# A planner's priorities and engine choices replaced by a table, in a two-layer hybrid attention trunk

## The chip, the core and the metric

One NeuronCore of a Trainium2 chip runs the whole program. The metric is the device time of one execution in microseconds (us); three runs of the kernel before gave 615.03, 615.44 and 615.48 us, a median of 615.44 us.

## What is computed

The input x is 256 tokens by 1024 channels. Each of two layers normalises x, multiplies it by one wide matrix (1024 by 9808), feeds the columns to three causal token mixers of eight heads each, and adds the merged result to x. A final RMSNorm ends the program. Cut to what matters:

```python
def hybrid_layer(x, gain, w_in, f_bias, w_branch, w_out):
    h = rms_norm(x, gain)
    proj = jnp.einsum('bsd,de->bse', h, w_in)
    (qa, ka, va, ga, qb, kb_, vb_, gb, qc, kc, vc, gc,
     q_idx, k_idx, w_idx, f_logit, merge_logit) = jnp.split(proj, SPLIT_POINTS, axis=-1)
    ...
    oa = moba_attention(rope(qa), rope(ka), va) * silu(ga)
    ob = dsa_attention(rope(qb), rope(kb_), vb_, qi, ki, wi) * silu(gb)   # top 64 keys of an indexer
    oc = forgetting_attention(qc, kc, vc, log_f) * silu(gc)
    y = jnp.einsum('nbsw,nwd->bsnd', jnp.stack([oa, ob, oc], axis=0), w_branch)
    merged = jnp.sum(sigmoid(merge_logit) * y, axis=2)
    return x + jnp.einsum('bsd,de->bse', merged, w_out)
```

With 256 tokens the block attention is plain causal attention over one block.

## The kernel before, in words

All matmuls keep nearly float32 accuracy: every operand is split into a high part (a rounding copy on ScalarE, L402) and a low part (source minus high on VectorE, L406), and each product is three matmuls: high by high, high by low, low by high (L444). Weights come from memory in chunks of up to 1 MB into four `raw` buffers, are split into rings of six `wh` and six `wl` buffers, and go to TensorE as the stationary operand, 128 columns at a time; one "unit" of 24 matmuls makes 128 output channels for all 256 tokens in one PSUM bank. Three banks (`proj`) take units, two (`s`) the attention scores, two (`t`) transposes, one (`o`) the attention outputs.

A layer's units come in this order: v of mixer a, v of mixer c with the index keys, the indexer (with eight rounds of top-8 on VectorE), the pairs of heads of mixer a, of mixer c, of mixer b, with merge gates (`m`) and branch products (`y`) put between them, and at the end the output projection. A pair of heads runs as a chain: scores (L665, L667), bias and row minimum on VectorE (L733, "max"), exp on ScalarE (L737), reciprocal (L740, L741, "recip"), a 16-bit high part of the probabilities (L745 on ScalarE or L748 on VectorE, "p hi"), its low part on VectorE (L752, "p lo"), a transpose by DMA from SyncE's queue (L761), a copy into `pt` (L766 on ScalarE or L767 on VectorE, "pT"), the product with v (L779 to L782, "av"), the sum of its two halves (L795, L797), the gate (L800, "og", on VectorE or GpSimd) and a split (L434, L435). The gate itself is L693 (tanh on ScalarE) and L694 (VectorE, "g"); L694 also sets free the `proj` bank that its unit filled. L977 on VectorE or L978 on GpSimd adds a branch product to the accumulator.

Nothing is ordered at run time but by semaphores. A planner (`Plan.run`) walks through all 3226 operations once, when the program is built: each has a modelled cost, its dependencies, its buffers and a priority (`key`, the smaller the earlier; a unit's number is the base of its operations' keys). At each step it takes the engine that can start soonest and, among that engine's operations that can start within a slack of that moment (0 on TensorE, 110 ns on ScalarE and VectorE, 1500 ns on SyncE), the one with the smallest key. Where an operation may go to two engines (`ways`), it takes the one that ends sooner by its model, after a penalty (500 ns for VectorE at "p hi" and "pT"). The order that comes out is fixed for each engine; an engine that waits holds everything behind it. The transpose is modelled as T_ISSUE on SyncE's queue and T_LAND until the data may be read:

```python
plan.op([("SP", T_ISSUE, tr)], k_hi + k_lo, k_t, key, T_LAND, "pT", touch=[e, t16]).quick = 1400.0
```

At the start, SyncE loads the two halves of the first 128 tokens (`x0`, L998), weights of mixer a's v in eight pieces (`va0` to `va7`, L1057, keys -95 to -93.6) and the two halves of the second 128 tokens (`x1`, L998, keys -94.7 and -94.69). The second half's norm is a sum of squares (L517), a mean (L524), a power on GpSimd (L526), a scaling (L534, L537) and transposes on TensorE (L567).

Of the kernel before, what the change touches and what calls it, by code (L numbers as in the profile page):

```python
# [38 lines left out]
STEP = 24.0  # L39
SPLIT_LEAD = 2.0  # L40
P_SCALE = 32768.0
T_ISSUE = 1400.0
T_LAND = 1600.0
AWAY = 500.0
SLACK = {"PE": 0.0, "ACT": 110.0, "DVE": 110.0, "SP": 1500.0}
MARGIN = 200.0
# [41 lines left out]
    return c  # L88


SHIFT = {}


CUR = [""]
# [21 lines left out]
class Plan:  # L116
# [8 lines left out]
    def op(self, ways, reads, writes, key, lag=0.0, name="", touch=()):  # L125
        o = Op()
        o.ways, o.key, o.lag, o.name, o.margin, o.port, o.half, o.quick = ways, key, lag, name, 0.0, False, False, 0.0
        deps, o.bufs = {}, []
        for t in reads:
            for d in t.w:  # L130
                deps[id(d)] = d
        for t in writes:
            for d in t.w + t.r:
                deps[id(d)] = d
        for t in reads:
            t.r.append(o)
        for t in writes:
            t.w, t.r = [o], []
        for t in {id(t): t for t in list(reads) + list(writes) + list(touch)}.values():
            if isinstance(t, Buf):  # L140
                if t.no is None:
                    t.no = self.made[t.tag] = self.made.get(t.tag, -1) + 1
                t.left += 1
                o.bufs.append(t)
        o.deps = list(deps.values())
        o.n, o.out, o.need, o.end = len(self.ops), [], 0, None
        o.key += SHIFT.get(o.n, 0.0)
        for d in o.deps:
            if d is not o:
                d.out.append(o)  # L150
                o.need += 1
        self.ops.append(o)
        return o
# [111 lines left out]
def hybrid_trunk(ctx, tc, x, w_in, w_branch, w_out, final_gain, consts, out):  # L265
# [15 lines left out]
    def T(b):  # L281
        return b.slot[1]
# [388 lines left out]
    class Pair:  # L671
# [44 lines left out]
        def attend(self, key):  # L716
# [8 lines left out]
            for h in range(2):  # L725
# [34 lines left out]
                def tr(h=h, t16=t16):  # L760
                    nc.sync.dma_start_transpose(T(t16).rearrange("p (a b) -> p a b", a=6), w16()[:, 768 * h:768 * h + 768])  # L761
                plan.op([("SP", T_ISSUE, tr)], k_hi + k_lo, k_t, key, T_LAND, "pT", touch=[e, t16]).quick = 1400.0
                for i in range(2):
# [497 lines left out]
```

## Time and profile before

| what | value |
|---|---|
| runs, median of 3 | 615.44 us |
| the profiled execution, its own time | 613.8 us |
| span in that profile | 612.0 us |
| TensorE busy | 595.2 us (97%) |
| VectorE busy | 543.9 us (89%) |
| ScalarE busy | 471.8 us (77%) |
| GpSimd busy | 87.2 us (14%) |

The span is the profiled part of that execution, 1.8 us shorter than its time. Matmuls overlap in the array, so their busy time counts nearly every instant in which one is under way; it hides waits that are shorter than a matmul's own length. In the rows a name such as `proj<-hTh,wh` says what is written and what is read; "idle before <-X" names the operation whose end released the instruction.

### The profile page before, as it was taken

Reading aid. Unit: us, or ns where it says so; the run is one execution under the profiler, and the core shown is the slowest. Engines: PE = TensorE matmul, PEld = TensorE weight load, DVE = VectorE, ACT = ScalarE, POOL = GpSimd, SP = SyncE. Lnnn points to the kernel's source line nnn. Section 1 sums busy time; section 2 is a strip of 40 time slices with the busy share of each in tenths; the row PEclk is TensorE's granted clock in tenths of the full one; section 3 lists DMA queues with packets and bytes.
Section 4 is the critical chain, followed back from the end, with each engine's and each line's share of the span. In section 5 each row is a group of like instructions: output and inputs, shape, how many; then the busy total and the mean of one; then the engine's idle time right before and its main releaser. Section 6 shows DMA issues by size and latency. Waiting matters only on the chain.

```text
span 612.0 us, 12689 instructions
## 1 busy us (share of the span) xinstructions
PE 595.2 (97%) x4704; PEld 570.4 (93%) x4704; DVE 543.9 (89%) x1342; ACT 471.8 (77%) x1028; POOL 87.2 (14%) x96
## 2 busy tenths in 40 slices
PE   8999999999999999999999999999999999999995
PEld 6899999989898999999889999999999899999985
DVE  8889998988798999899685999999989988999783
ACT  5768668988897779896395775799989876999741
POOL 1013142000000333200000420520000014221000
PEclk9999999999999999999999999999999999999999
DMA  9986285688586746478746645585957696464911
GB/s 314 297 271 189 74 271 110 186 204 263 103 276 170 226 140 168 125 191 309 227 138 207 207 139 159 172 219 128 322 160 224 136 276 195 113 194 88 344 34 70
DMA packets 136509, 116.83 MB, mean 191 GB/s; under 512 B 42752, under 2 KB 127360, under 8 KB 136448
## 3 DMA queue, kind: packets, MB, share of 16 engines
q1 hardware_dynamic: 136160, 115.59, 64.7%
q8 instruction: 37, 0.61, 0.4%
q10 hardware_dynamic: 288, 0.43, 0.2%
q14 instruction: 24, 0.20, 0.1%
HBM read 103.42 MB, written 1.05 MB: 171 GB/s over the span
## 4 chain that ended last, share of the span: by engine, by line
PE 33%; DVE 32%; ACT 19%; DMA 7%; issue 6%; POOL 2%; SPq 0%; POOLq 0%; DVEq 0%; ACTq 0%
PE proj L444 25%; DVE wl L406 10%; ACT wh L402 6%; DMA t<-e 5%; PE proj L1131 4%; DVE e L752 4%; ACT e L737 3%; DVE rsh L493 2%; DVE e L733 2%; DVE isc L907 2%; DVE isc L928 2%; DVE rr L495 1%; ACT pt L766 1%; DMA raw<-in_w_branch_dram 1%; DVE t L927 1%
## 5 line engine op out<-in xcount | busy, mean ns | idle before, releaser
L444 PE MATMUL proj<-hTh,wh 128*128 128x256 f32 x1024 | 266.3, 278 | 0.7 <-DVE bd0l L824 0.2
L444 PE MATMUL proj<-hTl,wh 128*128 128x256 f32 x1024 | 265.2, 277 | 0.0
L406 DVE TENSOR_TENSOR wl<-raw,wh 128x1024 fp32r<-128x1024 f32 x180 | 224.4, 1258 | 13.6 <-ACT wh L402 12.0
L444 PE MATMUL proj<-hTh,wl 128*128 128x256 f32 x1024 | 229.3, 277 | 0.0
L402 ACT ACTIVATE wh<-raw 128x1024 fp32r<-128x1024 f32 x180 | 187.1, 1055 | 37.1 <-PE proj L444 28.6
L444 PEld LDWEIGHTS proj<-hTh,wh 128*128 128x128 f32 x1024 | 192.2, 188 | 2.5 <-DVE g L694 1.3
L444 PEld LDWEIGHTS proj<-hTl,wh 128*128 128x128 f32 x1024 | 192.2, 188 | 0.1
L444 PEld LDWEIGHTS proj<-hTh,wl 128*128 128x128 f32 x1024 | 173.4, 188 | 0.0
L494 POOL TENSOR_TENSOR rsh<-rsh,cst 128x256 f32<-128x256 f32 x40 | 30.1, 752 | 378.7 <-DVE rsh L493 311.6
L496 POOL TENSOR_TENSOR rr<-rr,rsh 128x256 f32<-128x256 f32 x40 | 48.2, 1205 | 4.5 <-DVE rr L495 1.5
L766 ACT ACTIVATE pt<-t 128x384 fp32r<-128x384 f16 x78 | 37.0, 515 | 12.4 <-DMA t<-e 12.2
L737 ACT ACTIVATE e<-e,st 128x128 f32<-128x128 f32 x96 | 42.5, 444 | 2.1 <-DVE st L733 2.1
L752 DVE SCALAR_TENSOR_TENSOR e<-e,st 128x128 f16<-128x128 f32 x96 | 42.0, 437 | 1.0
L745 ACT ACTIVATE e<-e,st 128x128 f16<-128x128 f32 (+1 forms) x92 | 36.7, 443 | 2.4 <-DVE st L741 1.6
L444 PE MATMUL proj<-wh,v 128*128 128x512 f32 (+1 forms) x144 | 35.2, 366 | 0.0
L444 PE MATMUL proj<-og0l,wh 128*128 128x256 f32 x128 | 34.3, 279 | 0.6 <-DVE og0l L435 0.6
L444 PE MATMUL proj<-og0h,wh 128*128 128x256 f32 x128 | 32.9, 281 | 1.6 <-DVE g L694 1.6
L444 PEld LDWEIGHTS proj<-wh,v 128*128 128x128 f32 x144 | 25.3, 189 | 4.2
L444 PE MATMUL proj<-og0h,wl 128*128 128x256 f32 x128 | 28.8, 278 | 0.0
L444 PEld LDWEIGHTS proj<-og0h,wh 128*128 128x128 f32 x128 | 24.1, 188 | 2.1 <-DVE g L694 2.0
L444 PEld LDWEIGHTS proj<-og0l,wh 128*128 128x128 f32 x128 | 24.1, 188 | 1.0 <-DVE og0l L435 1.0
L797 DVE TENSOR_TENSOR ot<-o,ot 64x256 f32<-64x256 f32 x48 | 19.9, 414 | 2.4 <-ACT ot L795 2.0
(224 smaller groups left out, 1069.9 us busy)
## 6 DMA issues: line engine op xcount, KB each, us to landing
raw<-in_w_in_dram SPq DMA_DIRECT2D x74, 1024.0 KB, 5.7
raw<-in_w_branch_dram SPq DMA_DIRECT2D x24, 512.0 KB, 4.1
raw<-in_w_out_dram SPq DMA_DIRECT2D x8, 1024.0 KB, 8.4
raw<-in_x_dram SPq DMA_DIRECT2D x8, 256.0 KB, 5.0
tmp<-wf SPq DMA_DIRECT2D x16, 128.0 KB, 5.2
t<-e SPq DMA_TRANSPOSE x48, 2.8
raw<-in_w_in_dram SPq DMA_DIRECT2D x2, 320.0 KB, 7.6
x<-in_x_dram SPq DMA_DIRECT2D x2, 256.0 KB, 4.3
```

The costliest lines, as they stand in the source:

```text
L402: ACT.activation(p[0].v, sel(c.v), AF.Copy)
L406: DVE.tensor_tensor(p[1].v, sel(c.v), p[0].v.bitcast(F32), op=ALU.subtract)
L444: PE.matmul(o(), a(), b(), start=first and i == 0, stop=last and i == n - 1)
L493: dve(lambda: DVE.stream_shuffle(T(sh)[:np_], a(), SWAP), S, [ps], [sh], key, "rope")
L494: gps(lambda: POOL.tensor_tensor(T(sh)[:np_], T(sh)[:np_], s[:np_], op=ALU.mult), S, [k_rope], [sh], key, "rope")
L496: gps(lambda: POOL.tensor_tensor(T(r)[:np_], T(r)[:np_], T(sh)[:np_], op=ALU.add), S, [sh], [r], key, "rope")
L737: act(lambda t=t, a=a, n=n, st=st, h=h: ACT.activation(ex(h, a, n), ex(h, a, n), AF.Exp, bias=T(st)[:, t:t + 1], scale=-1.0, accum_out=T(s ...
L745: ACT.activation(hi(a, n), ex(h, a, n), AF.Copy, scale=T(st)[:, 4 + t:5 + t])
L752: dve(lambda t=t, a=a, n=n, st=st, h=h, hi=hi, lo=lo: DVE.scalar_tensor_tensor(lo(a, n), ex(h, a, n), T(st)[:, 4 + t:5 + t], hi(a, n), op0 ...
L766: plan.op([("ACT", t_act(384, False), lambda to=to, src=src: ACT.activation(to(), src(), AF.Copy)), ("DVE", t_dve2(384), lambda to=to, src ...
L797: dve(lambda r=r, h=h: DVE.tensor_tensor(T(t)[r], T(o)[:64, h * S:(h + 1) * S], T(t)[r], op=ALU.add), S, [o], [kt[h]], key, "og", touch=[t ...
L1131: PE.matmul(T(ps[t])[:, :w], hA[hi](a + x, t), T(p[wi])[:, ats[w > 256][wi]][:, :n * w].rearrange("p (k c) -> p k c", k=n)[:, x], start=le ...
```

## The change

Two constants of the planner's model of the transposes are smaller. A table SHIFT adds a number between -12 and +6 to the keys of 327 operations (255 earlier, 72 later), named by their number in the order in which the code makes them. A new table WAY adds -1500 or +1500 ns to the modelled cost on VectorE of 53 operations that have two ways: -1500 sends one to VectorE, +1500 to the other engine. No instruction is added or removed; the planner runs anew with these, so any place in any engine's order may move. Cut (the two tables to their first and last lines):

```diff
-T_ISSUE = 1400.0
-T_LAND = 1600.0
+T_ISSUE = 1250.0
+T_LAND = 1500.0
...
-SHIFT = {}
+SHIFT = {
+    0: -11.5, 1: -7, 3: -11.5, 4: -11, 17: 2, 28: -8, 31: -6, 47: -11, 73: 4, 80: -12, 89: -2.5, 90: -11.5, 91: 1.5,
+    98: -8, 99: -9.5, 100: 2.5, 188: 3, 308: -7, 310: -7, 364: 6, 380: 2.5, 386: -12, 387: -7, 419: 3.5, 440: -11,
...
+    2992: -3, 3009: -4, 3044: -12, 3046: -9, 3048: -8, 3076: -12, 3079: -11.5, 3127: -7, 3175: -12, 3177: 6, 3212: 5,
+}
+WAY = {
+    17: -1500, 18: -1500, 90: -1500, 99: 1500, 489: 1500, 490: 1500, 539: 1500, 552: -1500, 553: -1500, 559: 1500,
...
+    2802: 1500, 2827: 1500, 2841: 1500, 2846: -1500, 2852: 1500, 2940: 1500, 3009: -1500,
+}
...
         o.key += SHIFT.get(o.n, 0.0)
+        if len(ways) > 1 and o.n in WAY:
+            o.ways = [w + (WAY[o.n],) if w[0] == "DVE" else w for w in ways]
```

Operations that the prediction names: 0 and 1 are the loads of `x0`, 3 and 4 those of `x1`; 80, 89 and 98 those of `va1`, `va2` and `va3` (`va0`'s load is not in the table); 47 is the mean of the second half's norm; 478, 479, 1380, 1381, 2942 and 2943 are the "max" operations that free score banks at 92.9, 256 and 551 us; 1078, 1079, 2640 and 2641 are the gates "g" ahead of the last branch products of mixer a.

## Rows read from the trace of the kernel before

**Rows 1.** The page: busy time, share and instructions of each engine, and the TensorE clock that was granted, in tenths, over 40 equal slices.

```profile
PE 595.2 (97%) x4704; PEld 570.4 (93%) x4704; DVE 543.9 (89%) x1342; ACT 471.8 (77%) x1028; POOL 87.2 (14%) x96
PEclk9999999999999999999999999999999999999999
```

**Rows 2.** Busy time by stretch: the stretch and its length, then the busy time of each engine in it (with the number of instructions), the granted clock, the share of the DMA engines and their rate.

```profile
50.00:100.00 50.00, 49.38 (x427) 48.81 (x427) 49.03 (x153) 36.40 (x79) 11.91 (x13) 1.00 0.53 153
100.00:150.00 50.00, 48.32 (x414) 46.89 (x413) 45.67 (x105) 43.78 (x98) 3.81 (x4) 1.00 0.77 210
150.00:200.00 50.00, 47.49 (x373) 44.91 (x372) 43.23 (x122) 43.30 (x105) 0.00 (x0) 1.00 0.72 192
...
400.00:450.00 50.00, 49.78 (x437) 49.17 (x436) 47.00 (x106) 45.79 (x101) 3.82 (x4) 1.00 0.79 220
```

**Rows 3.** TensorE's waits: what waited for what, the idle time in us in total, how often, the longest.

```profile
PE o L779 <- ACT pt L766: 2.5, 4, 1.1
PE proj L444 <- DVE g L694: 1.6, 2, 0.8
PE s L665 <- DVE st L733: 1.5, 4, 0.5
PE t L567 <- ACT tmp L534: 1.3, 1, 1.3
...
PE proj L444 <- DVE og0l L435: 0.6, 1, 0.6
PE o L779 <- DVE ot L797: 0.5, 1, 0.5
PE o L781 <- ACT pt L766: 0.3, 1, 0.3
```

**Rows 4.** What a matmul of a unit takes by its record, from the page's groups of instructions (count, then total us and mean ns).

```profile
L444 PE MATMUL proj<-hTh,wh 128*128 128x256 f32 x1024 | 266.3, 278 | 0.7 <-DVE bd0l L824 0.2
```

**Rows 5.** How far matmuls of a unit stand apart when nothing holds them, from the chain that ended last in order of time: start in us, length in us, what, how many.

```profile
35.79 2.76 PE proj L444 x24
```

**Rows 6.** The timeline of the first 17 us, single lines: start, length, engine (SPq is SyncE's queue), line, operation, tiles, shapes, count, and in brackets the idle time before with its releaser.

```profile
0.74 0.87 SPq L998 DMA_DIRECT2D xg<-in_x_dram  x2
1.66 0.90 SPq L1057 DMA_DIRECT2D raw<-in_x_dram  x2
2.60 0.91 SPq L998 DMA_DIRECT2D x<-in_x_dram  x2
3.54 2.95 SPq L1057 DMA_DIRECT2D raw<-in_x_dram  x6
...
7.21 0.50 PE L1071 MATMUL proj<-wh,hTh 128*128 128x512 f32 x1
...
10.73 0.63 ACT L517 ACTIVATE acc<-x 128x512 f32<-128x512 f32 x1
...
14.22 0.15 DVE L524 SCALAR_TENSOR_TENSOR small<-small 128x1 f32<-128x1 f32 x1
...
16.15 0.44 PE L567 MATMUL t<-cst,tmp 128*128 128x128 f32 x2 [1.30 <-ACT tmp L534]
```

**Rows 7.** The page's busy rate of the DMA engines in the first slice of 15.3 us (GB/s, 40 slices).

```profile
GB/s 314 297 271 189 74 271 110 186 204 263 103 276 170 226 140 168 125 191 309 227 138 207 207 139 159 172 219 128 322 160 224 136 276 195 113 194 88 344 34 70
```

**Rows 8.** The timeline around the gate "g" and the branch product that waits for its bank, VectorE and TensorE.

```profile
188.71 0.41 DVE L694 SCALAR_TENSOR_TENSOR g<-th,proj 128x256 f32<-128x256 f32 x1
...
189.18 0.39 PE L444 MATMUL proj<-og0h,wh 128*128 128x256 f32 x1 [0.81 <-DVE g L694]
```

**Rows 9.** The transposes by DMA (L761): durations of their issue in ns, min/median/max, with first and last start, and the time from issue to landing over all 48.

```profile
L761 SPq DMA_TRANSPOSE t<-e x48: 1209/1222/2732, 96.3 to 562.3; - x48
...
DMA to landing us min/median/max: 2.7/2.8/7.1
```

**Rows 10.** Who waited for a transpose to land: idle us in total, times, longest.

```profile
ACT pt L766 <- DMA t<-e: 12.2, 10, 2.2
...
DVE pt L767 <- DMA t<-e: 4.8, 3, 2.5
```

**Rows 11.** Groups of instructions of the operations that can go to either engine: count, then total us and mean ns of one.

```profile
L766 ACT ACTIVATE pt<-t 128x384 fp32r<-128x384 f16 x78 | 37.0, 515 | 12.4 <-DMA t<-e 12.2
...
L745 ACT ACTIVATE e<-e,st 128x128 f16<-128x128 f32 x48 | 18.9, 394 | 2.4 <-DVE st L741 1.6 <-DVE st L740 0.6
...
L800 DVE TENSOR_TENSOR ot<-ot,g 128x256 f32<-128x256 f32 x24 | 10.7, 446 | 0.8
...
L767 DVE CAST pt<-t 128x384 fp32r<-128x384 f16 x18 | 6.1, 355 | 4.8 <-DMA t<-e 4.8
...
L748 DVE TENSOR_SCALAR e<-e,st 128x256 f16<-128x256 f32 x4 | 1.4, 350 | 0.1
```

**Rows 12.** The timeline of VectorE and GpSimd around 207 us: a weight split alone and two beside GpSimd's multiply and add.

```profile
205.79 1.22 DVE L406 TENSOR_TENSOR wl<-raw,wh 128x1024 fp32r<-128x1024 f32 x1
...
207.45 0.73 POOL L494 TENSOR_TENSOR rsh<-rsh,cst 128x256 f32<-128x256 f32 x1 [99.39 <-DVE rsh L493]
207.59 1.68 DVE L406 TENSOR_TENSOR wl<-raw,wh 128x1024 fp32r<-128x1024 f32 x1
208.27 1.61 POOL L496 TENSOR_TENSOR rr<-rr,rsh 128x256 f32<-128x256 f32 x1
...
209.87 1.78 DVE L406 TENSOR_TENSOR wl<-raw,wh 128x1024 fp32r<-128x1024 f32 x1
```

32 rows, old and new, of tables (SHIFT, WAY) are left out of this document.

## The prediction

> **What bounds the kernel now.** I read the page's busy times first. TensorE is busy for 595.2 of 612.0 us at the full clock throughout [rows 1], so neither the clock nor the amount of matmul work leaves much, and the change alters neither. What is left to an order is the time in which TensorE waits. The busy time hides part of that: a matmul's record is 278 ns long [rows 4], but 24 in a row take 2.76 us, 115 ns each [rows 5], so a wait shows as idle only beyond 278 - 115 = 163 ns, and each listed wait is really that much longer.
>
> The list of TensorE's waits [rows 3] then gives the prize. After the head there are the products with v waiting for the transposed probabilities on ScalarE (2.5 and 0.3 us, 5 times), branch products waiting for a gate (1.6, 2 times), scores waiting for the row minimum to free a score bank (1.5, 4 times), and two single waits at the split and the sum of mixer outputs (0.6 and 0.5). That is 7.0 us in 13 waits, with 13 x 0.163 = 2.1 us added 9.1 us. In the head one wait of 1.3 us, really 1.5 us, stands before the second half's transposes. Together 10.6 us: what an order that never lets TensorE wait there could win, and the floor of my range.
>
> Third I read the timeline at these waits. At 189 us a gate on VectorE ends at 188.71 + 0.41 and a branch product that needs its bank starts right behind it, 0.81 us late [rows 8]. In the head the second half's sum of squares ends its main instruction at 10.73 + 0.63 = 11.36 us, but the mean is issued at 14.22 us, because VectorE has it behind weight splits, and TensorE starts the transposes at 16.15 us [rows 6]. So these are matters of place in a queue, not of work. Last I read the stretches: between 100 and 200 us VectorE is busy for 88.9 of 100 us and ScalarE for 87.1, between 50 and 100 us VectorE for 49.03 of 50 [rows 2]; this says how much room a moved operation finds.
>
> **The change part by part.** No instruction is added, so the sum is over waits.
>
> *Head.* The mean (operation 47) gets -11 and both loads of x1 move up. By their keys the loads go x0, x0, va1, x1, x1, va3, va2, va0 in place of x0, x0, va0, va1, x1, x1, va2, va3. The first weight piece comes as early as now, the second two loads later. A load is 256 KB, at the 314 GB/s of the first slice [rows 7] 0.83 us, so the second piece comes 1.7 us later, at a time when the first one feeds TensorE with three matmuls only (about 0.7 us at 0.23 us each, twice the 115 ns of a matmul half as wide). Bounds: a loss of 1.0 us, if the later piece holds TensorE from 7.2 us on [rows 6], and a gain of 1.5 us, if the wait at 16.15 us goes whole. I take a gain of 1.0, nearer to the gain, since the mean has 2.9 us of queueing to give (14.22 - 11.36) and x1 comes one load earlier too.
>
> *Body, priorities.* The shifted operations lie where the waits are: the gates at 187 to 189 us and at 482 to 484 us have -6.5 and -12, the "max" operations that free the score banks at 92.9, 256 and 551 us -2.5 to -12, and many "recip", "p lo" and "pT" steps between 90 and 200 us are in the table. The waits that it addresses are those on the pT copies, on the gates and on the row minimum, the last in three of its four places, which I count as three quarters: 2.8 + 1.6 + 1.1 = 5.5 us in 10 waits, with 10 x 0.163 = 1.6 us added 7.1 us. The fourth score bank, the split and the sum of mixer outputs have no entry. Bounds: nothing, if every operation pulled forward only makes the one it passes late, and 7.1 us. An operation passed on VectorE is in most places a weight split for a unit several us away, which can bear it; but behind a wait that goes, the next dependency is seldom far. I take two thirds, 4.7 us.
>
> *Body, engines.* Laid along the static order, 34 of the 53 assignments name another engine than now: 12 pT copies and 10 "p hi" from ScalarE to VectorE, 2 pT copies the other way, 2 scalings in the head to VectorE, and 6 gates "og" and 2 accumulations to GpSimd. ScalarE loses 10 x 0.51 us of copies net and 10 x 0.39 us at least of "p hi", 9.0 us, and VectorE gains 10 x 0.355 + 10 x 0.35 = 7.1 us [rows 11], both where each has idle time [rows 2]; for TensorE that is nothing by itself. But VectorE now also waits for landings. A pT copy that waits for its transpose cost it 4.8 us in 3 times, 1.6 us each [rows 10], and 18 copies [rows 11] lead to 3 waits. Twelve more make 2 more waits, 3.2 us of VectorE with weight splits and gates queued behind them. Bounds: nothing, where VectorE is ahead, and 3.2 us. I take a third, 1.0 us lost, as VectorE keeps some lead in these stretches.
>
> *GpSimd.* The 8 moved operations take 0.45 us each on VectorE [rows 11], 3.6 us in all. A weight split takes 1.22 us alone and 1.68 or 1.78 us beside GpSimd [rows 12], 0.46 to 0.56 us more, so 8 such meetings cost 3.7 to 4.5 us: about nothing is won or lost, and I count nothing, between a gain of 3.6 us of VectorE (no meeting) and a loss of 0.9. The Trainium skill ("SBUF — State Buffer", section "Who interferes with whom") says that VectorE with two SBUF inputs and GpSimd reading SBUF exclude each other for a whole instruction. By it each move would hold VectorE for GpSimd's whole 0.73 us, 5.8 us in all, and a third of the net 2.2 us would put my time 0.7 us higher; the measured stretching is less, so I go by the rows.
>
> *The two constants.* They put a transpose at 1.25 + 1.5 = 2.75 us in place of 3.0 us; the measured landing is 2.7 at least, 2.8 in the median and 7.1 at most [rows 9]. They move the copies at most 0.25 us forward in the plan; I count nothing for the shortest landings and leave the late ones to the last rival.
>
> The sum: -1.0 - 4.7 + 1.0 = -4.7 us. Against the profiled execution that is 613.8 - 4.7 = 609.1 us; this execution was 1.6 us under the median of 615.4, so the median to expect is **610.7 us**.
>
> **The rivals.**
>
> *All waits go.* The order removes all listed waits: 615.4 - 10.6 = 604.8 us. For it: the shifts stand in the very places of the waits. Against it: three of the waits have no entry near them, and the landings up to 7.1 us do not follow a priority.
>
> *The waits only change places.* An order fixed at build time fits one set of landings and lengths; the gains are eaten by new waits of the same size, and the table does not do what it is for. 615.4, within 1.2 us of it. For it: VectorE at 49.03 of 50 us [rows 2] can't take up a lead from the head, and 7.1 us of work are added to it. Against: ScalarE and VectorE both have idle time in the stretches where most entries lie.
>
> *Slower: VectorE is held by transposes.* The 12 copies given to VectorE are of 9 transposes. If the landing is late for all of them, as an earlier place in the order and the 2.75 us under the median landing [rows 9] would make it, each holds VectorE for 1.6 us [rows 10], 14.4 us in all; half of it, 7.2 us, reaches TensorE through late weight splits and gates. The waits on pT copies then stay (2.8 + 5 x 0.163 = 3.6 us, of which I had counted two thirds, 2.4), so of my gains 5.7 - 2.4 = 3.3 us are left, and the time is 615.4 + 7.2 - 3.3 = 619.3 us. It decides from 3.3 / 9 = 0.4 us of TensorE per transpose on. For it: ScalarE already loses 12.2 us to landings, and a queue in order passes this on. Against: the copies can land later in VectorE's order too, and ScalarE's waits would shrink with them.
>
> **How the numbers follow.** The forecast of 610.7 us (606.5 to 613.8) gets 0.58, all waits gone 0.12, changed places 0.11, VectorE held 0.19. A measurement can tell about 0.2%, 1.2 us, from no change. Faster is the first two, 0.70; same 0.11; slower 0.19. The range goes from 604.3 us, just under the floor of the waits, to 617.5 us, where the head's loss of 1.0 us and some of the last rival are in and its worse part, about 0.1, is out. The forecast alone would span 606.5 to 613.8 us.
>
> **What would show it.** Right: the gates' waits of TensorE are gone, the waits on pT copies and on the row minimum are down to about a third, the mean in the head is issued before 12.5 us, TensorE's last matmul comes some 4 to 5 us earlier, VectorE's busy time is up by about 7 us and ScalarE's down by about 9. The prediction is wrong if the pT copies on VectorE wait over 10 us in all for landings, if the weight splits (L406) become what TensorE waits for, or if the head's first matmuls after 7.2 us stand waiting for a weight piece for over 1 us.

## The result, and the profile after

| | before | after |
|---|---|---|
| median of 4 runs each, same chip | 615.39 us (615.03 to 615.48) | 601.2 us (600.14 to 601.6) |
| the profiled execution: its time, its span | 613.8, 612.0 us | 601.2, 599.4 us |
| TensorE idle in the span | 612.0 - 595.2 = 16.8 us | 599.4 - 587.5 = 11.9 us |

The ratio is 0.9768, with a 95% interval of 0.9751 to 0.9785: 14.2 us faster, where 4.7 us were forecast. Between the two traces the difference is 12.6 us, because the profiled execution of before was 1.6 us under its median and that of after is at its own. The order and the engines of the operations are all that differs; in the code after, lines stand 42 further down (L486 was L444, L821 was L779).

The first lines of the page of after, answering to [rows 1], and of its chain of waits, shares by engine (before it was PE 33%, DVE 32%, ACT 19%, DMA 7%):

```profile
PE 587.5 (98%) x4704; PEld 567.8 (95%) x4704; DVE 542.3 (90%) x1360; ACT 463.8 (77%) x1004; POOL 92.4 (15%) x102
PEclk9999999999999999999999999999999999999999
PE 58%; DVE 22%; ACT 9%; DMA 5%; issue 4%; POOL 0%; SPq 0%; POOLq 0%; DVEq 0%; ACTq 0%
```

The same 4704 matmuls at the same clock have 7.7 us less busy time (595.2 to 587.5), and the idle time fell by only 4.9 us. More than half of the gain thus lies inside what the profile counts as busy. How waits get there can be seen in the busy time by stretch; first before, then after, columns as in [rows 2]:

```profile
0.00:20.00 20.00, 17.55 (x77) 13.54 (x78) 16.10 (x48) 12.82 (x33) 1.81 (x8) 1.00 0.96 317
20.00:100.00 80.00, 79.38 (x658) 78.25 (x657) 75.29 (x199) 57.52 (x117) 18.11 (x20) 1.00 0.66 196
100.00:200.00 100.00, 95.81 (x785) 91.80 (x784) 88.90 (x226) 87.08 (x202) 3.81 (x4) 1.00 0.74 201
```

```profile
0.00:20.00 20.00, 18.54 (x87) 15.43 (x88) 17.83 (x52) 12.43 (x29) 2.06 (x8) 1.00 0.94 313
20.00:100.00 80.00, 80.00 (x677) 79.65 (x676) 74.62 (x208) 58.27 (x118) 19.80 (x22) 1.00 0.67 202
100.00:200.00 100.00, 98.07 (x813) 95.07 (x812) 93.57 (x233) 88.90 (x200) 6.37 (x6) 1.00 0.76 204
```

From 20 to 100 us TensorE was busy for 79.38 of 80 us, so by that column an order could win 0.62 us there; measured by the distances between matmul starts (below), TensorE lost 1.3 us in it before and 0.3 us after. (The counts in brackets, 658 and 677, are not of the same matmuls, as TensorE after is 2.3 us ahead at 20 us.) The timeline of before at 123 us shows how a wait hides. Columns: start, length, engine, line, operation, tiles, shapes, count:

```profile
123.43 0.28 PE L444 MATMUL proj<-hTl,wh 128*128 128x256 f32 x1
123.55 0.28 PE L444 MATMUL proj<-hTh,wl 128*128 128x256 f32 x1
123.94 0.38 PE L444 MATMUL proj<-hTh,wh 128*128 128x256 f32 x1
```

The first two starts are 0.12 us apart, the normal distance [rows 5]; the third comes 0.39 us after the second, so TensorE lost 0.28 us there, but the record of the matmul before fills all of it except 0.11 us, and the row has no bracket with an idle time at all. I therefore took, from all matmul starts in order, each distance less the undisturbed one for that width (0.113 us for 256 columns, 0.058 for 128, 0.226 for 512) and kept what was over 0.07 us. The head is counted from the first transposes on, which start at 6.3 us before and 6.6 us after; what stands ahead of them is warm-up products of `ones`. This is worked out from the traces, not a view of the page:

| time that TensorE lost, us (number of gaps) | before | after |
|---|---|---|
| head, the first 20 us | 4.0 | 1.4 |
| then gaps of 0.07 to 0.163 us, which leave no idle time | 5.0 (48) | 2.3 (22) |
| gaps of 0.163 to 0.3 us | 2.9 (12) | 0.3 (1) |
| gaps over 0.3 us | 9.7 (15) | 5.4 (8) |
| all | 21.6 | 9.3 |

(The entries are rounded one by one.) The difference of the sums, 12.2 us, is nearly the whole 12.6 us between the traces. By what stood waiting, over the whole span: products with v lost 6.7 us before and 2.2 after, branch products 3.6 and 1.6, scores 2.7 and 0.4.

TensorE's listed waits of after, answering to [rows 3]: what waited for what, us in total, times, longest.

```profile
PE proj L486 <- DVE mth L1017: 1.3, 1, 1.3
PE o L821 <- ACT pt L808: 1.1, 3, 0.5
PE t L1032 <- DVE ones L1027: 1.1, 1, 1.1
PE proj L486 <- ACT mth L986: 1.0, 1, 1.0
PE proj L486 <- DVE g L736: 0.3, 2, 0.2
```

The wait for the row minimum and the 1.3 us in the head are gone, that for the gate is down from 1.6 to 0.3 us, that for the pT copies from 2.8 to 1.1. Two single waits for a bank that had not been freed are new: for a merge gate's product with a branch product on VectorE (L1017, 1.3 us) and for a merge gate's tanh on ScalarE (L986, 1.0 us).

The head, answering to [rows 6]: loads in the order x0, x0, va1, x1, x1, then the other pieces, and the mean (L566) at 7.95 us where it was at 14.22.

```profile
1.67 0.42 SPq L1099 DMA_DIRECT2D raw<-in_x_dram  x1
2.13 0.91 SPq L1040 DMA_DIRECT2D x<-in_x_dram  x2
...
7.95 0.15 DVE L566 SCALAR_TENSOR_TENSOR small<-small 128x1 f32<-128x1 f32 x1
```

Last the operations with a choice of engine, answering to [rows 10, 11]: two waits for landings, then groups (count, total us, mean ns, idle before):

```profile
ACT pt L808 <- DMA t<-e: 6.8, 4, 2.9
...
DVE pt L809 <- DMA t<-e: 1.2, 3, 0.7
```

```profile
L808 ACT ACTIVATE pt<-t 128x384 fp32r<-128x384 f16 x73 | 34.3, 513 | 7.1 <-DMA t<-e 6.8
L809 DVE CAST pt<-t 128x384 fp32r<-128x384 f16 x23 | 9.1, 412 | 1.3 <-DMA t<-e 1.2
L842 DVE TENSOR_TENSOR ot<-ot,g 128x256 f32<-128x256 f32 x18 | 7.7, 426 | 0.6
L841 POOL TENSOR_TENSOR ot<-ot,g 128x256 f32<-128x256 f32 x6 | 5.9, 978 | 32.0 <-DVE ot L839 31.9
L790 DVE TENSOR_SCALAR e<-e,st 128x256 f16<-128x256 f32 x10 | 3.4, 351 | 0.1
L790 DVE TENSOR_SCALAR e<-e,st 128x128 f16<-128x128 f32 x9 | 2.5, 282 | 0.0
```

VectorE has 5 more pT copies net and 15 more "p hi" (19 in place of 4), ScalarE as many fewer. Operation by operation 67 changed engine: 40 from ScalarE to VectorE, 17 the other way, 8 from VectorE to GpSimd and 2 back. The table differs from the order of before in 34; the planner moved the other 33 by itself when it ran anew.

The Trainium skill ("Perfetto Trace Analysis", section "Identifying the Most-Contended Engine") says that the busy share of matmuls is no good measure of what is left, and that the busy share of weight loads is one. These traces agree: weight loads left 612.0 - 570.4 = 41.6 us free before and 599.4 - 567.8 = 31.6 us after, 10.0 of the 12.6 us, where matmul idle time shows 4.9.

### The profile page after: what moved, and what is told of

Read it like the earlier page. It is cut to its first block, busy times and chain, and to the rows that moved or that the text cites. A ratio compares the mean times of both kernels' runs of the same rounds, so it can differ in the third digit from the quotient of the medians.

```text
span 599.4 us, 12672 instructions
## 1 busy us (share of the span) xinstructions
PE 587.5 (98%) x4704; PEld 567.8 (95%) x4704; DVE 542.3 (90%) x1360; ACT 463.8 (77%) x1004; POOL 92.4 (15%) x102
## 4 chain that ended last, share of the span: by engine, by line
PE 58%; DVE 22%; ACT 9%; DMA 5%; issue 4%; POOL 0%; SPq 0%; POOLq 0%; DVEq 0%; ACTq 0%
PE proj L486 47%; DVE wl L448 7%; PE proj L1173 4%; DMA t<-e 4%; ACT wh L444 2%; PE proj L1113 2%; DVE isc L970 2%; DVE e L794 1%; DVE rsh L535 1%; ACT pt L808 1%; ACT e L779 1%; DVE t L969 1%; DVE isc L949 1%; DMA raw<-in_w_out_dram 1%; DVE rr L537 1%
## 5 line engine op out<-in xcount | busy, mean ns | idle before, releaser
L486 PE MATMUL proj<-hTh,wh 128*128 128x256 f32 x1024 | 265.7, 278 | 1.5 <-ACT mth L986 1.0
L486 PE MATMUL proj<-hTl,wh 128*128 128x256 f32 x1024 | 265.0, 277 | 0.0
L448 DVE TENSOR_TENSOR wl<-raw,wh 128x1024 fp32r<-128x1024 f32 x180 | 223.3, 1249 | 15.2 <-ACT wh L444 14.0
L486 PE MATMUL proj<-hTh,wl 128*128 128x256 f32 x1024 | 227.9, 276 | 0.0
L444 ACT ACTIVATE wh<-raw 128x1024 fp32r<-128x1024 f32 x180 | 188.7, 1054 | 38.6 <-PE proj L486 26.3
L486 PEld LDWEIGHTS proj<-hTh,wh 128*128 128x128 f32 x1024 | 192.2, 188 | 2.3 <-ACT mth L986 1.2
L486 PEld LDWEIGHTS proj<-hTl,wh 128*128 128x128 f32 x1024 | 192.2, 188 | 0.0
L486 PEld LDWEIGHTS proj<-hTh,wl 128*128 128x128 f32 x1024 | 172.9, 188 | 0.0
L536 POOL TENSOR_TENSOR rsh<-rsh,cst 128x256 f32<-128x256 f32 x40 | 32.4, 812 | 351.4 <-DVE rsh L535 323.2
L538 POOL TENSOR_TENSOR rr<-rr,rsh 128x256 f32<-128x256 f32 x40 | 45.6, 1140 | 2.8
L779 ACT ACTIVATE e<-e,st 128x128 f32<-128x128 f32 (+1 forms) x96 | 42.6, 445 | 2.9 <-DVE st L775 2.4
L794 DVE SCALAR_TENSOR_TENSOR e<-e,st 128x128 f16<-128x128 f32 (+1 forms) x96 | 40.1, 424 | 1.1 <-ACT e L787 0.4
L808 ACT ACTIVATE pt<-t 128x384 fp32r<-128x384 f16 x73 | 34.3, 513 | 7.1 <-DMA t<-e 6.8
L486 PE MATMUL proj<-wh,v 128*128 128x512 f32 (+1 forms) x144 | 35.2, 366 | 0.0
L486 PE MATMUL proj<-og0l,wh 128*128 128x256 f32 x128 | 33.8, 277 | 0.0
L486 PE MATMUL proj<-og0h,wh 128*128 128x256 f32 x128 | 32.4, 278 | 1.3 <-DVE mth L1017 1.3
L787 ACT ACTIVATE e<-e,st 128x256 f16<-128x256 f32 (+1 forms) x77 | 31.6, 445 | 2.7 <-DVE st L783 2.3
L486 PEld LDWEIGHTS proj<-wh,v 128*128 128x128 f32 x144 | 25.3, 189 | 4.3
L486 PE MATMUL proj<-og0h,wl 128*128 128x256 f32 x128 | 28.6, 276 | 0.0
L486 PEld LDWEIGHTS proj<-og0h,wh 128*128 128x128 f32 x128 | 24.0, 188 | 1.6 <-DVE mth L1017 1.5
L486 PEld LDWEIGHTS proj<-og0l,wh 128*128 128x128 f32 x128 | 24.0, 188 | 0.0
L486 PEld LDWEIGHTS proj<-og0h,wl 128*128 128x128 f32 x128 | 21.7, 188 | 0.0
```

What stands on the lines that cost most here:

```text
L444: ACT.activation(p[0].v, sel(c.v), AF.Copy)
L448: DVE.tensor_tensor(p[1].v, sel(c.v), p[0].v.bitcast(F32), op=ALU.subtract)
L486: PE.matmul(o(), a(), b(), start=first and i == 0, stop=last and i == n - 1)
L536: gps(lambda: POOL.tensor_tensor(T(sh)[:np_], T(sh)[:np_], s[:np_], op=ALU.mult), S, [k_rope], [sh], key, "rope")
L538: gps(lambda: POOL.tensor_tensor(T(r)[:np_], T(r)[:np_], T(sh)[:np_], op=ALU.add), S, [sh], [r], key, "rope")
L779: act(lambda t=t, a=a, n=n, st=st, h=h: ACT.activation(ex(h, a, n), ex(h, a, n), AF.Exp, bias=T(st)[:, t:t + 1], scale=-1.0, accum_out=T(s ...
```

## The experiments

My theory after the result: the gain is many small waits of TensorE, spread over the span, and it adds up stretch by stretch as TensorE gets ahead. The rivals: one stretch makes it (the head above all); one part of the change makes it (shifts, engines or constants); any other order would have done as well; a single distance, from the scores to the product with v, makes it. An expectation that calls theories by a letter or a number says beside it what each forecasts.

Most of these kernels have the planner's choice replaced by a written order. This common edit is shown once; in it an operation's number is its place in the order of creation, as in the tables:

```diff
+ORDER = [...]
+RANK = {n: i for i, n in enumerate(ORDER)}
+ENGINE = {17: "DVE", 18: "DVE", ...}
+SHIFT = {}
+WAY = {}
...
-            for o in ready:
+            for o in sorted(ready, key=lambda q: RANK[q.n]):
...
+                if ok:
+                    break
...
+            w = next((w for w in o.ways if w[0] == ENGINE.get(o.n)), o.ways[0])
```

### By stretch

**Head of after, rest of before.** The order of after for the first 153 of the 3226 operations, that of before for the last 3068, a few between join the two; the engines go with the order.

```diff
-ORDER = <before: 1 to 3226>
+ORDER = <after: 1 to 153> + <5 between> + <before: 159 to 3226>
```

> The order of all engines is written down as a list: up to the last matmul of mixer a's v in the first layer it is the order of the changed kernel, from there on the order (and engine choices) of the kernel before. Theory 1 (the gain is places in queues, it adds up stretch by stretch, and a lead of TensorE is kept): the lead of 2.3 us that the changed kernel has at this point stays to the end, 615.4 - 2.3 = 613.1 us (612.3 to 614). Rival (VectorE, busy 49 of 50 us in the indexer's stretch, can't keep up with a lead): the lead is gone by 100 us and the time is that of the kernel before, 615.4 us (over 614.6).

Measured: 612.31 against 614.39 us, ratio 0.996 (0.9944 to 0.9976), 2.1 us faster. By the medians the head's lead is mostly kept to the end, but it is a small part of the gain. The trace, of the longest of its ten runs, has a lead of 1.3 us at 20 us and none at the end, so this rests on the times alone.

**The reverse: head of before, rest of after.**

```diff
-ORDER = <after: 1 to 3226>
+ORDER = <before: 1 to 161> + <3 between> + <after: 165 to 3226>
```

> The other half: the order of the kernel before up to the last matmul of mixer a's v in the first layer, from there on the order of the changed kernel. Theory 1 (stretches add up): 601.2 + 2.3 = 603.5 us (602.5 to 604.5). Rival (the lead of the head is lost to VectorE in the indexer's stretch): 601.2 us as the changed kernel (under 602).

Measured: 602.61 us, ratio 0.9805 (0.9789 to 0.9821). Against the ratio of after, 0.9768, the old head costs 0.0037 x 615 = 2.3 us. The two runs agree on the head's part, and the rest, some 12 us, lies in the body.

**One stretch in the middle.** The order of after from place 484 to 1193, about 84 to 212 us, in the order of before.

```diff
-ORDER = <before: 1 to 3226>
+ORDER = <before: 1 to 483> + <after's order of the 710 operations there> + <before: 1194 to 3226>
```

> Order of the kernel before up to 84 us, of the changed kernel from there to where it stands at 203 us (the pairs of mixers a and c of the first layer and the v of mixer b), then of the kernel before again. Theory 1 (adds up): the changed kernel wins 5.5 us between these points, so 615.4 - 5.5 = 609.9 us (608.5 to 611.5), and the waits of TensorE on pT copies and gates are gone there alone. Rival (the gain needs the order before and after it, because buffers and loads come due differently): most of it is lost at the two seams, over 613 us.

Measured: 610.70 us against 614.39, ratio 0.9944 (0.9929 to 0.9959); by the ratio 3.4 us faster, by the medians 3.7. In the pair of traces before and after, TensorE's lead at equal matmul work (worked out by laying the two orders of matmuls side by side) grows by 5.5 us in this stretch, by 2.3 in the head, about 2.0 from 212 to 312 us and 2.8 behind that, in the second layer. Put in alone the stretch first loses about 1.5 us by 120 us, and then wins its 5.5; 0.7 us of that is lost behind the second seam. That the loss comes from the front seam, where the operations of before leave a different state, was not tried. So the stretches add as far as they were run alone, the head and this one, and the theory of many places stands; the 4.8 us of the rest were only read from the pair of traces.

**Another order of the same kind.** The same 327 shifts and 53 ways, dealt out anew among the same operations, with the new constants.

```diff
-SHIFT = {0: -11.5, 1: -7, 3: -11.5, 4: -11, 17: 2, 28: -8, ...
+SHIFT = {0: -7.5, 1: -1, 3: -12, 4: -11.5, 17: -8, 28: -12, ...
-WAY = {17: -1500, 18: -1500, 90: -1500, 99: 1500, ...
+WAY = {17: -1500, 18: 1500, 90: -1500, 99: -1500, ...
```

> The changed kernel with the values of both tables dealt out anew at random among the same entries (the same 327 operations get the same set of shifts in another order, the same 53 the same set of signs). Theory 1 (each value says which operation goes ahead of which): the gain is gone, 612 to 622 us. Rival (the order before is simply an unlucky one and any new draw of the plan near these places is better): 600 to 608 us.

Measured: 628.13 us, ratio 1.0227 (1.0211 to 1.0242), above either range. It is one draw, but it speaks against the rival: the values matter, operation by operation. TensorE's listed waits there are longer (L782 of this kernel is L779 of before, L447 is L444):

```profile
PE o L782 <- DVE ot L800: 4.8, 2, 4.5
PE proj L447 <- DVE g L697: 3.8, 2, 2.5
```

Not all of the 13.7 us are waits. In this trace the granted clock is at 0.5 from 10.6 and from 280.3 us for 3.41 us each, and from 447.5 us for 10.24 us, in and behind the longest wait; by the distances between starts this costs some 5 us. All four runs have a mean clock of 0.984 to 0.988, where those of before have 0.997 to 0.999.

### By part

**Shifts alone**, the constants of before and no WAY:

```diff
-T_ISSUE = 1250.0
-T_LAND = 1500.0
+T_ISSUE = 1400.0
+T_LAND = 1600.0
...
-WAY = {17: -1500, ...
+WAY = {}
```

> Planned anew with the shifted priorities alone: no engine table, T_ISSUE and T_LAND as before. Theory 1 (places in queues carry the gain and the three parts can be had apart): most of it stays, 603 to 607 us. Theory 2 (the parts were chosen together: the plan goes astray at the first place where an operation takes the other engine): 610 to 625 us, no better than the kernel before.

**Ways alone**, the constants of before and no SHIFT:

```diff
-SHIFT = {0: -11.5, ...
+SHIFT = {}
```

> Planned anew with the engine table alone: no shifted priorities, constants as before. Theory 1: engine choices by themselves are worth little, 613 to 616 us. Rival (relief of ScalarE is what counts): 604 to 610 us. Theory 2 (parts chosen together): 614 to 625 us.

**Constants alone**, both tables empty:

```diff
-SHIFT = {0: -11.5, ...
-WAY = {17: -1500, ...
+SHIFT = {}
+WAY = {}
```

> Planned anew with T_ISSUE 1250 and T_LAND 1500 alone, both tables empty. Theory 1: the copies' places move little, 612 to 618 us. Theory 2 (any new plan is a new draw): anywhere between 610 and 628 us, and not near 601.

**Both tables, the constants of before:**

```diff
-T_ISSUE = 1250.0
-T_LAND = 1500.0
+T_ISSUE = 1400.0
+T_LAND = 1600.0
```

> Both tables as in the changed kernel, but T_ISSUE 1400 and T_LAND 1600 as before. Theory 1 (the constants by themselves are worth nothing, the tables carry the gain): 600 to 604 us. Theory 2 (table and constants were chosen together, the plan strays without them): 604 to 612 us.

| in the planner | us | ratio (95%) |
|---|---|---|
| shifts alone | 603.67 | 0.9815 (0.9799 to 0.9832) |
| ways alone | 611.72 | 0.9952 (0.9934 to 0.9969) |
| constants alone | 621.4 | 1.0102 (1.0079 to 1.0124) |
| shifts and ways | 608.06 | 0.9885 (0.9866 to 0.9904) |
| all three | 601.2 | 0.9768 (0.9751 to 0.9785) |

Shifts alone came out as theory 1 had it, constants alone and both tables as theory 2, and ways alone in none of the ranges. The parts don't add. Ways alone win 3.0 us, put on top of the shifts they lose 608.06 - 603.67 = 4.4; the constants alone lose 6.6 us, put on top of both tables they win 608.06 - 601.2 = 6.9. The tables fit the planner with the new constants, not the chip by themselves. Of the constants' 6.6 us about 1.5 are again clock: it is at 0.5 for 3.41 us from 148.0 us on, behind TensorE waits of 1.8 and 0.6 us.

**The order of after with the engines of before**, as lists:

```diff
 ORDER = <after: 1 to 3226>
-ENGINE = {17: "DVE", 18: "DVE", 19: "ACT", ... 46: "DVE", ...
+ENGINE = {17: "ACT", 18: "ACT", 19: "ACT", ... 46: "ACT", ...
```

> The changed kernel's order written down as a list, but each operation with two engines on the one it had in the kernel before (67 of them go back, the table's and those that the planner moved by itself). Theory 1 (places in queues): most of the gain stays, 602 to 607 us. Rival (the balance of the engines carries a good part): 608 to 616 us, with waits on pT copies back in the two stretches from 90 to 190 us and from 390 to 480 us.

**The order of before with the engines of after:**

```diff
-ORDER = <after: 1 to 3226>
+ORDER = <before: 1 to 3226>
 ENGINE = {17: "DVE", 18: "DVE", 19: "ACT", ... 46: "DVE", ...
```

> The order of the kernel before as a list, each operation with two engines on the one that it has in the changed kernel (67 differ). Theory 1 with what order-only showed (order and engine belong together): no better than before, 614 to 622 us. Rival (the engine choices alone are worth 3 us, as planned anew): 611 to 613 us.

Measured: order alone 614.14 us, ratio 0.9995 (0.997 to 1.0021), its runs from 612.22 to 620.18; engines alone 623.78 us, ratio 1.0134 (1.0108 to 1.016); the first as the rival in its text had it, the second above either range. Together they are 14.2 us faster, one by one nothing and 9.0 us slower. The trace of the first is of its longest run, so it shows the places and not the size; the new waits are for merge gates and pT copies on ScalarE (in this and the following kernels lines stand 165 further down than before: L944 is L779, L609 is L444), while those of the second are mostly for score banks and gates:

```profile
PE proj L609 <- ACT mth L1109: 4.1, 4, 1.4
PE o L944 <- ACT pt L931: 2.9, 2, 2.5
```

```profile
PE s L830 <- DVE st L898: 3.3, 5, 1.0
PE proj L609 <- DVE g L859: 2.8, 5, 1.1
```

The spread of the order alone has a cause that its trace shows: the clock is at 0.5 for 3.41 us from 9.9, 115.7 and 143.0 us on, the last behind a TensorE wait of 2.5 us, which costs some 4 us. Its ten runs go by the mean granted clock: 612.22 to 613.48 us at 0.994 to 0.999 (five), 614.80 to 616.86 us at 0.991 (four), 620.18 us at 0.988. In the five the order alone is about 2 us faster than before, still far from 14.2.

**The 8 operations that went to GpSimd sent back to VectorE**, all else as after:

```diff
-ENGINE = {... 559: "POOL", ... 1240: "POOL", ... 1290: "POOL", ...
+ENGINE = {... 559: "DVE", ... 1240: "DVE", ... 1290: "DVE", ...
```

> The changed kernel's order as a list, with the six gates og and the two accumulations that it gives to GpSimd back on VectorE at the same places of the list. If GpSimd's share of the port costs VectorE what the move frees (0.45 us freed, 0.46 to 0.56 us lost for each where they meet): 601.2 us within 1 us. Rival (the move frees VectorE where it is late): 602.5 to 605 us.

Measured: 601.68 us, ratio 0.9781 (0.9765 to 0.9797), the same as after within the intervals, as in the first of the two forecasts.

### By mechanism

From the scores to the product with v of the same pair there were mostly 11 to 17 us before and 13 to 27 us after (one pair went from 16.0 to 27.2 us): the product stands further back in TensorE's order, so its transposes and copies have longer. Is this distance the cause?

**Before, with eight products with v three places later** among TensorE's operations. One of the eight as an example, a number to a line:

```diff
-    694,
...
     800,
+    694,
```

> The order of the kernel before as a list, with one kind of edit: on TensorE the eight products with v that waited over 0.15 us in its trace (6.6 us in all, inside and before them) stand three quarter units (about 2.0 us) later; all other engines keep their order but for two neighbours. Theory A (the distance between scores and product with v is what the changed kernel adds, and TensorE can fill it): 4 to 5 us of the 6.6 go, 615 - 4.5 = 610.5 us (609 to 612). Theory B (the chain behind the product, its sums, gates and splits, holds VectorE and ScalarE by as much, since their places in those queues stayed): 613.5 to 617 us; with it, the order of all engines must move together.

Measured: 615.24 us against 614.89, ratio 1.0003 (0.999 to 1.0016): nothing. Yet the edit did what it was for. By the distances between matmul starts the products with v lost 0.7 us in place of 6.7, but branch products 5.4 in place of 3.6, scores 4.4 for 2.7, and the units of mixer c's keys and gates 2.1 and 1.5 for 0.8 each: together 6.0 us won and 5.5 us lost again. The listed waits:

```profile
PE proj L609 <- DVE g L859: 1.8, 3, 0.8
PE s L830 <- DVE st L898: 1.7, 4, 0.5
...
PE proj L609 <- DVE qy L600: 1.2, 1, 1.2
...
PE o L944 <- ACT pt L931: 0.4, 1, 0.4
```

The product waits no more, TensorE reaches the next unit sooner, and there the gate, the row minimum or a split is late, as theory B had it: the other engines had not been put in an order that is as far ahead.

**After, with all 24 products with v three places earlier:**

```diff
     872,
+    694,
...
-    694,
```

> The changed kernel's order as a list, with all 24 products with v three quarter units (about 2.0 us) earlier on TensorE and nothing else changed. Theory A (the distance from scores to product is what covers the transposes, and the changed kernel uses it fully): in its trace the copies end 0.9 us ahead of the product in the middle, so most products then wait 1 to 2 us, and 615 us or more results (610 to 622). Rival (the changed kernel has distance to spare): 601 to 604 us.

Measured: 606.02 us, ratio 0.9868 (0.9826 to 0.9911), 4.8 us over after by the medians and 6.2 by the ratios (one of its four runs took 609.70 us, at a mean clock of 0.993). That is between the two ranges: less than theory A had, more than the rival.

```profile
PE o L944 <- ACT pt L931: 4.3, 4, 1.4
```

By the starts, products with v lose 8.7 us in place of 2.2, and 10 of the 24 have all of that. So the longer distance is used, and 14 of the products have these three places to spare. It is needed for a part of the gain and, by the run before, not enough.

### Single operations moved by hand

What is left after is seen at 562 us, in the timeline of ScalarE, VectorE and TensorE:

```profile
561.17 2.01 ACT L444 ACTIVATE wh<-raw 128x1024 fp32r<-128x1024 f32 x2 [2.29 <-DMA raw<-in_w_out_dram]
```

```profile
562.26 1.23 DVE L448 TENSOR_TENSOR wl<-raw,wh 128x1024 fp32r<-128x1024 f32 x1 [2.84 <-ACT wh L444]
563.40 0.75 DVE L1017 SCALAR_TENSOR_TENSOR mth<-mth,proj 128x256 f32<-128x256 f32 x2
```

```profile
563.87 0.39 PE L486 MATMUL proj<-og0h,wh 128*128 128x256 f32 x1 [1.34 <-DVE mth L1017]
```

A weight split waits for a load, VectorE waits 2.84 us for the split's high part, and the merge gate's product that frees a bank is behind it, though the last matmul of the branch product that it needs had ended at 560.5 us; TensorE pays 1.34 us. Such a place can be mended by one move.

**Seven moves by hand**, each of which takes an operation that waits out of the way of one that TensorE needs:

```diff
-3160,
...
 3109,
+3160,
```

(and 758 behind 709, 872 behind 692, 742 behind 503, 2434 behind 2255, 1402 behind 1400, 2126 behind 1999)

> The changed kernel's order as a list with seven operations put at other places: on VectorE one output weight split behind two branch products that free banks (TensorE waits 1.5 us there in the changed kernel), one rotary product ahead of two og sums (0.45), one weight split behind a gate (0.35); on ScalarE four weight copies behind the merge gates (1.2) or the pT copies (0.6, 0.6, 0.35) that TensorE waits for. Theory 1 (each of these waits is a place in a queue and goes with it, with two thirds kept): 5.0 us at the seven places, 3.3 us won, 597.9 us (596.5 to 599.5). Rival (another wait takes each place): 600.5 to 602 us.

Measured: 603.18 us, ratio 0.9803 (0.9783 to 0.9822): no gain over after, rather a loss, and outside both ranges. The largest new wait is for a transpose:

```profile
127.00 1.76 SPq L559 DMA_DIRECT2D raw<-in_w_in_dram  x1
129.31 1.27 SPq L926 DMA_TRANSPOSE t<-e  x1
...
135.06 0.52 ACT L931 ACTIVATE pt<-t 128x384 fp32r<-128x384 f16 x1 [1.61 <-DMA t<-e]
```

Its copy starts 135.06 - 129.31 = 5.75 us after the transpose was issued, about twice the median landing of 2.9 us, and ScalarE waits 1.61 us for it with all its later work; TensorE's product with v waits 2.0 us. The 1 MB load of weights ahead of the transpose is not new, though. The moves are on ScalarE and VectorE alone, and in after the same load stands ahead of the same transpose, which lands 5.8 us after its issue there too:

```profile
126.30 0.58 SPq L436 DMA_DIRECT2D raw<-in_w_in_dram  x1
127.87 1.22 SPq L803 DMA_TRANSPOSE t<-e  x1
```

What is new is that the transpose is issued 1.44 us later: the queue is 0.7 us later already ahead of that load, and the load's issue takes 1.76 us in place of 0.58. Why it does was not tried. By TensorE's starts the trace lost 3.2 us around there, and only half of it is the wait. The rest is the clock, seen in the stretch behind the wait; first after, then this run, columns as in [rows 2]:

```profile
137.00:141.00 4.00, 4.00 (x37) 4.00 (x37) 3.95 (x10) 3.80 (x8) 0.00 (x0) 1.00 0.84 267
```

```profile
137.00:141.00 4.00, 4.00 (x23) 4.00 (x23) 3.67 (x6) 3.84 (x10) 0.00 (x0) 0.57 0.74 213
```

The granted clock is at 0.5 for 3.41 us from 137.13 us on, and matmuls of 256 columns start 0.213 us apart there in place of 0.113: 23 start in a stretch that held 37, with TensorE busy throughout in both. That costs about 1.6 us.

**Three of these moves kept** (3160, 758, 742), three products with v (504, 694, 2256) one place later, and that load put behind the transpose:

```diff
-924,
...
 691,
+924,
```

> The changed kernel's order as a list with other edits than the first try: the output weight split behind two branch products on VectorE, two weight copies on ScalarE behind what TensorE waits for, three products with v (they wait 0.85, 0.75 and 0.58 us) one quarter unit later, and one 1 MB load on SyncE's queue behind the transpose that it stands ahead of. Theory A (waits go where the released place is no transfer): 1.5 + 1.1 + 2.2 us at these places, two thirds kept: 601.2 - 3.2 = 598.0 us (597 to 599.7). Theory B (each gives a new wait as in the first try): 601 to 603.5 us.

Measured: 599.85 us (598.99 to 600.97), ratio 0.9756 (0.9738 to 0.9774), the lowest of all kernels here, 1.3 us under after by the medians, 0.7 us by the ratios, and just above theory A's range. The intervals overlap, so that it beats after isn't shown. Its order of SyncE and its waits:

```profile
125.48 4.10 SPq L926 DMA_TRANSPOSE t<-e  x2
129.63 0.56 SPq L559 DMA_DIRECT2D raw<-in_w_in_dram  x1
```

```profile
PE proj L609 <- DVE g L859: 0.9, 2, 0.7
PE proj L609 <- ACT mth L1109: 0.6, 1, 0.6
```

The transpose lands 2.8 us after its issue now, and the clock stays at 1.00 up to 594 us, behind the last matmul. The 1.3 us wait at 562 us is gone (no wait for VectorE's merge-gate product is listed). How much of the step from 603.18 to 599.85 us is the load, and how much the moves left out, was not taken apart; the wait and the clock at 137 us went together.

## Why the prediction was wrong

The sign and the order of the mechanism were right, the size was not: 601.2 us measured, 610.7 forecast, and below the range. The 9.5 us between them, by the prediction's steps: 5.9 in the body, 1.6 in the head (2.6 by the gaps less 1.0; its first transposes start 0.3 us later, so that the lead is 2.3), 1.6 in the step from the trace to the median, 0.4 unassigned.

*The prize: the step that failed.* I summed the listed idle waits, added 0.163 us to each, and called 9.1 us in the body and 1.5 in the head all that an order could win, "the floor of my range". I had the rule in hand that a wait shorter than 0.163 us leaves no idle time, and used it to lengthen the waits that I saw, not to ask how many I didn't. The starts of the matmuls give 17.6 us lost in the body of before (5.0 + 2.9 + 9.7) and 4.0 in the head. The listed waits of the body are the 15 long gaps, 9.7 us, of which my 13 with 9.1 us were sized well; 60 shorter ones with 7.9 us, none long enough to be listed, were missing. So the prize was 17.6 us in the body and not 9.1, and no floor stood at 604.8 us. Of the long ones 44% went (9.7 to 5.4), of the short ones 67% (7.9 to 2.6).

*The share.* I took two thirds of the body waits with an entry, 4.7 us, and 1.0 off for engines. The body won 17.6 - 8.0 = 9.6 us. The share of two thirds was too high for the long waits and right for the short ones; what was wrong is what it was a share of. 5.5 of the 12.6 us come between 84 and 212 us, where the listed waits are thickest. And what I held against the change, that VectorE is busy for 49.03 of 50 us from 50 to 100 us [rows 2], is no bar: after, it is busy as long (49.36 us), and TensorE is busy for 50.00 of 50 us there, 0.62 us more.

*The head.* Forecast 1.0 us, measured 2.1 and 2.3 us in two runs. The mechanism was as written: the mean left the queue (7.95 us), the wait at 16.15 us went, the later weight piece cost at most the 0.5 us by which TensorE is behind at 8 us, before it is 2.3 us ahead at 20 us. The bound of 1.5 us was the same failed step: the head had 4.0 us of gaps.

*The engines.* The forecast was 1.0 us lost, VectorE up by 7 us, ScalarE down by 9. ScalarE fell by 8.0. VectorE fell too, by 1.6 (543.9 to 542.3). By its records, which overlap a little, 15 "p hi" and 5 copies net brought 7.7 us, as forecast in size though not in number, and six gates took 3.1 away; the rest is that the records of its other operations are shorter, by some 5 to 6 us in all (weight splits 224.4 to 223.3 us), of which I show no cause. I had counted the table's 34 and not the 33 that the planner would move itself. Waits for landings fell on both engines, ScalarE 12.2 to 6.8 us and VectorE 4.8 to 1.2, so the rival in which VectorE is held by transposes did not come about; and the engine moves are no cost to be taken off but a part without which the order is worth about 2 us.

*GpSimd* was counted at nothing, and sending its 8 operations back changes nothing that can be measured: right. Its prices were chance: 0.46 and 0.56 us are what was left of GpSimd's instruction, less 0.13 us, when those two splits began (last section).

*The constants* were counted at nothing. Alone they lose 6.6 us, with the tables they win 6.9, so that was wrong: I asked which landings they are nearer to, and not what else in the order they move.

*The median.* I added the 1.6 us by which the trace of before lies under its median. After's trace is at its median (601.2 both), so that step shifted the forecast the wrong way by as much.

## What to carry to other kernels

Measure what a static order can win on a saturated TensorE by the distances between matmul starts, or by the free time of its weight loads, stretch by stretch: idle time showed 16.8 us with the head's start in it, where gaps of 21.6 us could be worked on. An order, the engines and the planner's model belong together: taken apart here, each piece was worth between -11 and +9 us, and mending one wait on one engine (three places of slack for the products with v) gave back nearly all it won. A long wait can cost more than its length: read the granted clock behind it before a loss is put down to waits alone. Single moves by hand are worth trying last, and a large load that stands ahead of a transpose in SyncE's queue is worth a look among them.

## What the runs showed of the hardware

The copy of a transposed tile took VectorE 412 ns in the mean after (23 of them) and 355 before (18) [rows 11], the same shape. The lengthening goes with GpSimd: after, the 18 that met no instruction of GpSimd took 354 ns, the 5 that did 342 to 902 ns, 622 in the mean.

A weight split that begins while GpSimd works on a multiply or an add took 1.08 us and what was left of GpSimd's instruction, but never under the 1.21 us that it takes alone: before, 1.68 us with 0.59 left (at 207.59 us), 1.75 with 0.68 (at 44.11), 1.21 with 0.05 (at 40.63). The other way round GpSimd's add took 1.61 us when it began during such a split (at 208.27 us), and 0.74 where it met none. So the two kept each other out for nearly a whole instruction, which the prediction had set aside. A gate product of the same shape took GpSimd 978 ns and VectorE 426 ns, and it still cost nothing to put six of them there.

A transpose issued behind a 1 MB load landed late, 5.8 us after its issue in after and 5.7 in the first version with moves by hand; with the load behind it, 2.8 us, where the median is 2.9.

In four of the traces (shuffled tables, constants alone, order alone, the first moves by hand) the granted clock fell to 0.5 for 3.41 us at a time, once for 10.24. Behind the head each such stretch follows or begins in a TensorE wait of 0.6 us or more, but not each long wait has one: in the trace of shifts alone 1.9 us at 246 us has none. What sets it off was not tried.
